# Attention scores of a head pair issued in one place, on two halves of TensorE's rows

## The chip, the cores and the metric

The kernel runs on one core of a Trainium2 chip. The metric is the device time of one execution in microseconds (us); smaller is better. Five engines work beside each other and wait for each other through semaphores: TensorE (PE, matrix products, with its weight loads shown as PEld), VectorE (DVE), ScalarE (ACT), GpSimd (POOL) and SyncE (SP, which issues the DMAs here). Products land in PSUM, which has eight banks of 128 partitions by 512 fp32 values.

## The reference, cut to what matters

The program computes two model blocks, one after the other, on 512 tokens of width 1024. The change concerns only the first mixer of the first block, an attention by "stick breaking" with 16 heads of width 64:

```python
q, k, v = jnp.split(h @ w_in, 3, axis=-1)            # 512 x 1024 each, 16 heads of 64
for start in range(0, seq, QBLK):                    # QBLK = 128: four blocks of queries
    end = start + QBLK
    z = jnp.einsum('bhtd,bhsd->bhts', qf[:, :, start:end], kf[:, :, :end]) * scale
    earlier = jnp.arange(end)[None, :] < jnp.arange(start, end)[:, None]
    log_keep = jnp.where(earlier, jax.nn.log_sigmoid(-z), 0.0)
    csum = jnp.cumsum(log_keep, axis=-1)
    log_w = jax.nn.log_sigmoid(z) + (csum[..., -1:] - csum)
    w = jnp.where(earlier, jnp.exp(log_w), 0.0)
    outs.append(jnp.einsum('bhts,bhsd->bhtd', w, vf[:, :, :end]))
```

Everything else (cross attention, feed-forward, the three branches of the second block) is the same before and after, and takes more than four fifths of the time.

## The kernel before

**Numbers in two parts.** All large products run with fp32 operands that are split into a high part (rounded to fp32r) and a low part (the rest). `mm3` sums three products: high by high, low by high, high by low. A split costs one ACT copy (high) and one subtraction, on DVE mostly (low).

**Pairs of heads.** The attention goes through eight pairs `hp` of heads. For each pair, two GEMMs over xT (24 matmuls of 512 columns each, `chunk`) give q and k of both heads, transposed: head e stands in rows `hrow(e)`, 64 rows each. Four `gemm_v` per two pairs give the values. `gemm_q` writes one tile per head, with the head's high part in its own 64 rows and its low part in the other 64. `gemm_k` writes per head a tile with the high part in both halves, and another with the low part in the head's own half and zeros in the other (`k_lo`). So one matmul over all 128 rows sums two of the three products, and a second one the third: 2 matmuls for a head and a block of queries (`scores`, line 482).

**The chain of a pair**, in the generator `attention` (line 480): scores (PE) into a PSUM bank, a sigmoid (`keep`, ACT), a cumulative product (`r`, a scan on DVE), the difference of neighbours (`w`, POOL); this five times (`weights_of`: block 1 of both heads together, then for each head blocks 0 and 2 together and block 3). Then 20 transposes of w on PE in five groups, each group followed by a split (`wth` on ACT, `wtl` on DVE); then 16 matmuls with v (`values`), and the sums of the two parts (`yt`, `y`), and their split.

**What sets the order.** Each engine runs its instructions in the order in which the program records them. The generator is run beside the GEMMs: `mm` counts the columns of the GEMM matmuls, and during the attention every 1650 ns of them by its own count (8 matmuls of 512 columns, 16 of 256) `tick` lets the generator go on to its next `yield`; the number that it yields (table `WAIT`, at0 to at5) is how many ticks it then waits. `tick` also calls `pump`, which issues the next load of weights (`wr`, two buffers) and records the conversion of the one loaded (`wh` on ACT, `wl` on DVE, lines 144 and 145). Attention of pair hp runs beside the GEMMs of pair hp+1: beside q, k and then two `gemm_v` where hp is 0, 2 or 4; beside two `gemm_v`, q and k where hp is 1, 3 or 5. `drain` finishes it before the next begins. Pair 6 runs beside q and k of pair 7, and pair 7 beside GEMMs over `memT` (256 columns, split into `kT`); there pair 6's rest is not drained first, so the two pairs overlap.

**PSUM.** Eight banks in four rings: g (3 banks, GEMMs), a (2), b (2), c (1).

## Time and profile before

| | |
|---|---|
| median of 3 runs | 1349.75 us (1348.98 to 1350.78) |
| the profiled execution | 1349.54 us, of which the span of the trace is 1347.8 us |
| TensorE busy | 1322.6 us, 98% of the span |
| granted TensorE clock | full in every slice of the page |
| attention (with its GEMMs) | from the start to about 222 us |

A busy PE is not a PE at its peak: matmuls are pipelined, and the duration of one (272 to 400 ns) holds a tail that the next one covers. What a matmul costs in a stream is the distance from its start to the start of the next one, and that is how the rows below are to be read.

### The profile page before, as it was taken

The numbers are of one execution on the slowest core, as the hardware profiler recorded it, in microseconds if no ns is written. First come the engines' busy times: TensorE is split into PE (matmuls) and PEld (weight loads), VectorE is DVE, ScalarE is ACT, GpSimd is POOL, SyncE is SP. The second block draws the span as 40 slices with busy tenths as digits, with TensorE's granted clock in tenths as the row PEclk, the third lists the DMA queues.
The fourth block names the chain that finished last, engine by engine and source line by source line (L and its number), as shares of the span: only waits on it lengthen the run. The fifth ranks groups of instructions, "written<-read, shape, count | busy, mean of one in ns | idle before, by whom it ended". The sixth has DMA issues, their size and how long they took to land.

```text
span 1347.8 us, 19442 instructions
## 1 busy us (share of the span) xinstructions
PE 1322.6 (98%) x7804; PEld 1108.6 (82%) x7804; DVE 833.7 (62%) x1428; ACT 527.2 (39%) x780; POOL 248.1 (18%) x241
## 2 busy tenths in 40 slices
PE   8999999999999999999999989999999989999997
PEld 7988888778879888888888888888877768887886
DVE  5787887865577665523456775767235666743575
ACT  6565665144423533421345136443222454222230
POOL 1433432000000433310133121200000442000220
PEclk9999999999999999999999999999999999999999
DMA  5221343242223322232234212233222223322341
GB/s 191 64 91 53 103 153 125 79 155 96 78 79 111 124 94 94 94 109 94 94 125 141 78 63 94 75 111 98 91 79 79 71 77 93 110 94 68 110 152 63
DMA packets 54666, 133.25 MB, mean 99 GB/s; under 512 B 19632, under 2 KB 21552, under 8 KB 54576
## 3 DMA queue, kind: packets, MB, share of 16 engines
q1 hardware_dynamic: 54576, 132.01, 30.2%
q8 instruction: 61, 1.00, 0.3%
q14 instruction: 29, 0.24, 0.1%
HBM read 126.48 MB, written 5.24 MB: 98 GB/s over the span
## 4 chain that ended last, share of the span: by engine, by line
PE 85%; DVE 9%; ACT 3%; issue 1%; DMA 1%; POOL 0%; DVEq 0%; SPq 0%; ACTq 0%; POOLq 0%
PE ps_chunk L214 48%; PE ps_rows L214 9%; PE ps_d L214 6%; PE ps_br L214 5%; PE ps_v L214 4%; PE ps_lead L214 3%; DVE wl L145 2%; PE ps_s L488 1%; PE ps_o L542 1%; DVE lnt L650 1%; PE ps_t L510 1%; PE ps_z L214 1%; PE ps_o L214 1%; DVE rs_t L279 1%; PE ps_w L1214 1%
## 5 line engine op out<-in xcount | busy, mean ns | idle before, releaser
L145 DVE TENSOR_TENSOR wl<-wr,wh 128x1024 fp32r<-128x1024 f32 x196 | 255.6, 1305 | 141.2 <-ACT wh L144 140.5
L144 ACT CAST wh<-wr 128x1024 fp32r<-128x1024 f32 x196 | 204.8, 1046 | 114.4 <-PE ps_d L214 51.2
L214 PE MATMUL ps_chunk<-h3Tl,wh 128*128 128x512 f32 x480 | 124.6, 395 | 0.0
L214 PE MATMUL ps_chunk<-h3Th,wh 128*128 128x512 f32 x480 | 124.5, 395 | 0.0
L214 PE MATMUL ps_chunk<-h3Th,wl 128*128 128x512 f32 x480 | 124.5, 396 | 0.0
L872 DVE SCALAR_TENSOR_TENSOR c<-ps_chunk,colp,c 128x511 f32<-128x511 f32 x80 | 59.9, 749 | 87.8 <-ACT c L870 86.4
L878 POOL TENSOR_TENSOR c<-c 128x512 f32<-128x512 f32 x21 | 42.4, 2021 | 363.4 <-ACT c L877 209.0
L214 PEld LDWEIGHTS ps_chunk<-h3Th,wh 128*128 128x128 f32 x480 | 89.0, 188 | 20.1 <-issue 1.5
L214 PEld LDWEIGHTS ps_chunk<-h3Th,wl 128*128 128x128 f32 x480 | 89.8, 189 | 19.0 <-issue 0.2
L214 PEld LDWEIGHTS ps_chunk<-h3Tl,wh 128*128 128x128 f32 x480 | 89.1, 188 | 19.3 <-issue 0.8
L214 PE MATMUL ps_chunk<-h2Th,wh 128*128 128x512 f32 x320 | 79.1, 389 | 0.0
L214 PE MATMUL ps_chunk<-h2Tl,wh 128*128 128x512 f32 x320 | 79.0, 389 | 0.0
L214 PE MATMUL ps_chunk<-h2Th,wl 128*128 128x512 f32 x320 | 79.0, 389 | 0.0
L500 POOL TENSOR_TENSOR w<-r 128x511 f32<-128x511 f32 x40 | 58.7, 1468 | 84.7 <-DVE r L498 75.9
L870 ACT ACTIVATE c<-ps_chunk,colp 128x512 f32<-128x512 f32 x40 | 31.1, 778 | 110.3 <-PE ps_chunk L214 110.3
L214 PEld LDWEIGHTS ps_chunk<-h2Tl,wh 128*128 128x128 f32 x320 | 60.1, 188 | 12.5
L214 PEld LDWEIGHTS ps_chunk<-h2Th,wl 128*128 128x128 f32 x320 | 60.1, 188 | 12.5
L214 PEld LDWEIGHTS ps_chunk<-h2Th,wh 128*128 128x128 f32 x320 | 60.0, 188 | 12.4
L498 DVE TENSOR_TENSOR_SCAN r<-keep,masks 128x512 f32<-128x512 f32 x40 | 59.8, 1509 | 12.5 <-ACT keep L496 8.0
L214 PE MATMUL ps_chunk<-xTh,wh 128*128 128x512 f32 x128 | 35.4, 401 | 4.8 <-ACT xTh L376 4.8
L214 PE MATMUL ps_d<-wh,gvb 128*128 128x512 f32 x128 | 39.8, 389 | 0.0
L496 ACT ACTIVATE keep<-ps_s 128x512 f32<-128x512 f32 (+1 forms) x48 | 24.5, 525 | 37.8 <-PE ps_s L488 37.8
(397 smaller groups left out, 2611.0 us busy)
## 6 DMA issues: line engine op xcount, KB each, us to landing
wr<-in_w_in_dram SPq DMA_DIRECT2D x65, 512.0 KB, 3.5
wr<-in_w_ff_dram SPq DMA_DIRECT2D x44, 512.0 KB, 3.5
wr<-in_w_dn_dram SPq DMA_DIRECT2D x22, 512.0 KB, 3.4
wr<-in_w_qk_dram SPq DMA_DIRECT2D x14, 512.0 KB, 3.5
wr<-in_w_br_dram SPq DMA_DIRECT2D x12, 512.0 KB, 3.4
wr<-in_w_v_dram SPq DMA_DIRECT2D x8, 512.0 KB, 3.5
wr<-in_w_xk_dram SPq DMA_DIRECT2D x8, 512.0 KB, 3.9
wr<-in_w_o_dram SPq DMA_DIRECT2D x8, 512.0 KB, 3.4
```

The lines of the kernel that those rows point to most:

```text
L144: A.copy(w.hi, raw)
L145: lo_of.tensor_tensor(w.lo, raw, f32(w.hi), ALU.subtract)
L214: T.matmul(ps, l, r, start=start, stop=stop)
L279: V.scalar_tensor_tensor(t, y, nv, y, ALU.mult, ALU.mult)
L488: T.matmul(ps[:, o:o + n], q[e][:, tok(i)], part[:, 0:n], start=z == 0 and o == 0, stop=z == 1 and i == parts[-1][1])
L496: A.activation(keep[:, j * n:(j + 1) * n], ps[:, 0:n], AF.Sigmoid, scale=-0.125)
L498: V.tensor_tensor_scan(r[:, ::-1], keep[:, ::-1], masks[:, m, ::-1], 1.0, ALU.mult, ALU.max)
L500: G.tensor_tensor(t[:, 0:S - 1], r[:, 1:S], r[:, 0:S - 1], ALU.subtract)
L510: T.transpose(ps[:, n], src[:, o + j * P:o + (j + 1) * P], ident)
L870: A.activation(c, ps, AF.Identity, scale=cw(2), bias=col("ffb", j))
L872: V.scalar_tensor_tensor(c[:, 2 - r:S], ps[:, 0:S - 2 + r], cw(r), c[:, 2 - r:S], ALU.mult, ALU.add)
L878: (V if end else G).tensor_tensor(cv, cg, cv, ALU.mult)
```

## The change

- `gemm_qk` replaces `gemm_q` and `gemm_k`: one split of the whole chunk, 128 rows at a time, into a high and a low tile. Nothing is stacked or doubled, and the zeroed `k_lo` tiles are gone.
- `scores` takes one head's 64 rows as they are, and so needs three matmuls for a head and a block (high by high, high by low, low by high) where two did. The heads take turns: each matmul of head 0, on rows 0 to 63 of the array, is followed by the same one of head 1, on rows 64 to 127, into another bank.
- All scores of a pair are recorded in one place, into six banks (a, a, b, b, c, g). The five sigmoids, scans and differences are recorded there too, one behind the other, where two to three GEMM groups lay between them before.
- The transposes come in two places, 8 and 12 (before 8, 4 and 8), and both heads' values in one, in banks c and g.
- `WAIT`: five ticks between scores and transposes, one between the two places of transposes, two before the values.

```diff
@@ -60,7 +60,7 @@
     "quant": 1550, "turn1": 7, "turn2": 6, "sn0": 1, "sn1": 4, "sn2": 5, "sn3": 3, "st0": 5, "st1": 4, "st2": 5, "st3": 4,
     "gate": 4, "p1": 2, "p2": 5, "p3": 4, "p4": 4, "ac": 2, "tk": 2, "inv": 1, "invn": 2, "pw0": 4, "pw1": 4,
     "pw2": 6, "pw3": 7, "mx": 4, "ysp": 1, "gl": 1, "xc": 14, "x1": 1, "x2": 2, "x3": 2, "so": 2, "mp": 2, "pp": 3,
-    "ss": 2, "us": 3, "ye": 4, "yo": 3, "yt": 1, "at0": 1, "at1": 1, "at2": 1, "at3": 1, "at4": 1,
+    "ss": 2, "us": 3, "ye": 4, "yo": 3, "yt": 1, "at0": 1, "at1": 1, "at2": 5, "at3": 1, "at4": 2,
     "at5": 2, "mh0": 2, "mh1": 3, "mh2": 1, "mh3": 2, "mh4": 1, "mix": 2, "as7": 2, "qa": 1650, "as": 1,
 }
 
@@ -429,37 +429,13 @@
         G.affine_select(out=masks[:, m, o:o + P], in_=masks[:, m, o:o + P], pattern=[[-1, P]],
                         compare_op=ALU.is_gt, fill=1.0, base=0, channel_multiplier=1)
 
-    def qk_tile(name):
-        return att("qk", 7, name, dt=F32R)
-
-    k_lo = [at.tile([P, S], F32R, name=f"kl{e}") for e in range(2)]
-    for e in range(2):
-        A.mul(k_lo[e][hrow(1 - e)], masks[hrow(1 - e), 0], 0.0)
-
-    def gemm_q(ps=None):
+    def gemm_qk(ps=None):
 
         if ps is None:
             ps = chunk(xT)
-        q = [qk_tile("q") for _ in range(2)]
-        for e in range(2):
-            A.copy(q[e][hrow(e)], ps[hrow(e)])
-        for e in range(2):
-            own = hrow(e)
-            V.tensor_tensor(q[e][hrow(1 - e)], ps[own], f32(q[e][own]), ALU.subtract)
-        return q
-
-    def gemm_k(ps=None):
-
-        if ps is None:
-            ps = chunk(xT)
-        k = [Split(qk_tile("kh"), lo) for lo in k_lo]
-        for o in range(2):
-            for e in range(2):
-                A.copy(k[e].hi[hrow((e + o) % 2)], ps[hrow(e)])
-        for e in range(2):
-            own = hrow(e)
-            V.tensor_tensor(k[e].lo[own], ps[own], f32(k[e].hi[own]), ALU.subtract)
-        return k
+        s = Split(att("qk", 8, "qkh", dt=F32R), att("qk", 8, "qkl", dt=F32R))
+        split_from(ps, s.hi, s.lo)
+        return s
 
     vws = []
 
@@ -480,13 +456,17 @@
     def attention(hp, q, k, vs):
         w, wT = {}, {}
 
-        def scores(e, *parts):
-
-            for z, part in enumerate((k[e].hi, k[e].lo)):
-                for ps, i, o in parts:
+        def scores(tags, *parts):
+
+
+            pss = [bank(t, "ps_s") for t in tags]
+            for z, (l, r) in enumerate(((q.hi, k.hi), (q.hi, k.lo), (q.lo, k.hi))):
+                for i, o in parts:
                     n = (i + 1) * P
-                    T.matmul(ps[:, o:o + n], q[e][:, tok(i)], part[:, 0:n],
-                             start=z == 0 and o == 0, stop=z == 1 and i == parts[-1][1])
+                    for e in range(2):
+                        T.matmul(pss[e][:, o:o + n], l[hrow(e), tok(i)], r[hrow(e), 0:n],
+                                 start=z == 0 and o == 0, stop=z == 2 and i == parts[-1][0])
+            return pss
 
         def weights_of(pss, m):
 
@@ -511,51 +491,34 @@
                 wT.setdefault((e, j), (s, n))
             split_from(ps.rearrange("p a b -> p (a b)"), s.hi, s.lo)
 
-        pss = [bank("a", "ps_s") for _ in range(2)]
+        pss = [scores(*parts) for parts in (("aa", (1, 0)), ("bb", (0, 0), (2, P)), ("cg", (3, 0)))]
+        t = weights_of(pss[0], 2)
+        w[0, 1], w[1, 1] = (t, 0), (t, 256)
         for e in range(2):
-            scores(e, (pss[e], 1, 0))
-        t = weights_of(pss, 2)
-        w[0, 1], w[1, 1] = (t, 0), (t, 256)
-        yield wait["at0"]
-        for e in range(2):
-            ps = bank("a", "ps_s")
-            scores(e, (ps, 0, 0), (ps, 2, P))
-            t = weights_of([ps], 0)
+            t = weights_of(pss[1][e:e + 1], 0)
             w[e, 0], w[e, 2] = (t, 0), (t, P)
-            yield wait["at0"]
-            ps = bank("a", "ps_s")
-            scores(e, (ps, 3, 0))
-            w[e, 3] = (weights_of([ps], 1), 0)
-            yield wait["at1"] if e == 0 else wait["at2"]
-
-        def values(e):
-            ps = bank("ca"[e], "ps_o")
-            steps = []
-            for j in range(4):
-                s, n = wT[e, j]
-                wid = (4 - j) * P
-                lhs = vs[j][:, hp % 2, 2 * e:2 * e + 2, :].rearrange("p a d -> p (a d)")
-                steps += [(z, j, lhs, part[:, n * P:n * P + wid]) for z, part in enumerate((s.hi, s.lo))]
-            steps.insert(3, steps.pop(7))
-            steps.insert(6, steps.pop(7))
-            for z, j, lhs, part in steps:
-                T.matmul(ps[:, j * P:S], lhs, part, start=(j == 0 and z == 0), stop=j == 2 and z == 1)
-            own, oth = hrow(e), hrow(1 - e)
-            A.copy(tmp[own], ps[oth])
-            V.tensor_tensor(y[own], ps[own], tmp[own], ALU.add)
-
+            w[e, 3] = (weights_of(pss[2][e:e + 1], 1), 0)
+        yield wait["at2"]
         group("b", [(0, i, 0) for i in range(4)])
         group("b", [(0, 1, 1), (0, 2, 1), (0, 3, 1), (0, 3, 3)])
         yield wait["at3"]
         group("a", [(0, 2, 2), (0, 3, 2), (1, 2, 2), (1, 3, 2)])
-        yield wait["at3"]
+        group("a", [(1, 1, 1), (1, 2, 1), (1, 3, 1), (1, 3, 3)])
         group("b", [(1, i, 0) for i in range(4)])
-        group("a", [(1, 1, 1), (1, 2, 1), (1, 3, 1), (1, 3, 3)])
+        yield wait["at4"]
         y, tmp = att("y", 1, "y"), att("keep", 2, "yt")
-        yield wait["at4"]
-        values(0)
-        yield wait["at5"]
-        values(1)
+        order = [(z, j) for j in range(4) for z in range(2)]
+        order.insert(3, order.pop(7))
+        order.insert(6, order.pop(7))
+        for e in range(2):
+            ps = bank("cg"[e], "ps_o")
+            for z, j in order:
+                s, n = wT[e, j]
+                T.matmul(ps[:, j * P:S], vs[j][:, hp % 2, 2 * e:2 * e + 2, :].rearrange("p a d -> p (a d)"),
+                         (s.hi, s.lo)[z][:, n * P:n * P + (4 - j) * P], start=(z, j) == (0, 0), stop=(z, j) == order[-1])
+            own, oth = hrow(e), hrow(1 - e)
+            A.copy(tmp[own], ps[oth])
+            V.tensor_tensor(y[own], ps[own], tmp[own], ALU.add)
         split_to(y, yT.hi[:, hp], yT.lo[:, hp])
 
     memT = bigt("memT", [P, 2, KC, M])
```

On PE, the scores of pair 1 in the stretch where the attention of pair 1 starts beside `gemm_v` of pair 2. Before (`q` holds high and low of one head, `kh` and `kl` the two tiles of k):

```order
L214 MATMUL ps_v<-wh,xTh 128x256 x8
L488 MATMUL ps_s<-kh,q 128x256
L488 MATMUL ps_s<-kl_158,q 128x256
L488 MATMUL ps_s<-kh,q 128x256
L488 MATMUL ps_s<-kl_159,q 128x256
L214 MATMUL ps_v<-wl,xTh 128x256 x8
L214 MATMUL ps_v<-wh,xTl 128x256 x8
L488 MATMUL ps_s<-kh,q 128x128
L488 MATMUL ps_s<-kh,q 128x384
L488 MATMUL ps_s<-kl_158,q 128x128
L488 MATMUL ps_s<-kl_158,q 128x384
L214 MATMUL ps_chunk<-xTh,wh 128x512 x8
```

and now, where `qkh` and `qkl` are the high and low tiles of q and of k:

```order
L467 MATMUL ps_s<-qkl,qkh 128x256 x2
L467 MATMUL ps_s<-qkh,qkl 128x256 x2
L467 MATMUL ps_s<-qkh 128x128 x2
L467 MATMUL ps_s<-qkh 128x384 x2
L467 MATMUL ps_s<-qkl,qkh 128x128 x2
L467 MATMUL ps_s<-qkl,qkh 128x384 x2
L467 MATMUL ps_s<-qkh,qkl 128x128 x2
L467 MATMUL ps_s<-qkh,qkl 128x384 x2
L467 MATMUL ps_s<-qkh 128x512 x2
L467 MATMUL ps_s<-qkl,qkh 128x512 x2
L467 MATMUL ps_s<-qkh,qkl 128x512 x2
L214 MATMUL ps_chunk<-xTh,wl 128x512 x8
```

The 16 matmuls that stood in five places between GEMM groups are 24 in one, and "x2" is one matmul of each head.

On DVE, from the scores of pair 1 to its last subtraction for the values. Before (an `r` row is a scan; the listing calls it SCALAR_TENSOR_TENSOR):

```order
L498 SCALAR_TENSOR_TENSOR r<-keep,masks 128x512 x2
L477 TENSOR_TENSOR v<-ps_v,v 128x2x128
L498 SCALAR_TENSOR_TENSOR r<-keep,masks 128x512
L145 TENSOR_TENSOR wl<-wr,wh 128x1024
L498 SCALAR_TENSOR_TENSOR r<-keep,masks 128x512
L145 TENSOR_TENSOR wl<-wr,wh 128x1024
L498 SCALAR_TENSOR_TENSOR r<-keep,masks 128x512
L448 TENSOR_TENSOR q<-ps_chunk,q 64x512 x2
L233 TENSOR_TENSOR wtl<-ps_t,wth 128x512 x2
L145 TENSOR_TENSOR wl<-wr,wh 128x1024
L233 TENSOR_TENSOR wtl<-ps_t,wth 128x512 x3
```

and now:

```order
L478 SCALAR_TENSOR_TENSOR r<-keep,masks 128x512 x5
L453 TENSOR_TENSOR v<-ps_v,v 128x2x128
L145 TENSOR_TENSOR wl<-wr,wh 128x1024 x2
L233 TENSOR_TENSOR qkl<-ps_chunk,qkh 128x512
L233 TENSOR_TENSOR wtl<-ps_t,wth 128x512 x2
L145 TENSOR_TENSOR wl<-wr,wh 128x1024
L233 TENSOR_TENSOR wtl<-ps_t,wth 128x512 x3
```

Between the scans stood a split of v and two conversions of weights (`wl`); now these stand behind all five scans, and q's subtraction is one of 128 rows where it was two of 64.

On ACT, the same stretch. Before:

```order
L496 ACTIVATE keep<-ps_s 128x256 x2
L496 ACTIVATE keep<-ps_s 128x512
L476 CAST v<-ps_v 128x2x2x64
L496 ACTIVATE keep<-ps_s 128x512
L144 CAST wh<-wr 128x1024
L496 ACTIVATE keep<-ps_s 128x512
L144 CAST wh<-wr 128x1024
L496 ACTIVATE keep<-ps_s 128x512
L445 CAST q<-ps_chunk 64x512 x2
L232 CAST wth<-ps_t 128x512 x2
L144 CAST wh<-wr 128x1024
L232 CAST wth<-ps_t 128x512 x3
```

and now:

```order
L476 ACTIVATE keep<-ps_s 128x256 x2
L476 ACTIVATE keep<-ps_s 128x512 x4
L452 CAST v<-ps_v 128x2x2x64
L144 CAST wh<-wr 128x1024 x2
L232 CAST qkh<-ps_chunk 128x512
L232 CAST wth<-ps_t 128x512 x2
L144 CAST wh<-wr 128x1024
L232 CAST wth<-ps_t 128x512 x3
```

The conversions `wh` stood among the sigmoids; now two stand behind all of them, and the third still stands ahead of the last three `wth`.

## Rows read from the trace of the kernel before

**Rows 1.** The page: engines' busy us, share of the span, instructions.

```profile
PE 1322.6 (98%) x7804; PEld 1108.6 (82%) x7804; DVE 833.7 (62%) x1428; ACT 527.2 (39%) x780; POOL 248.1 (18%) x241
```

**Rows 2.** Stretches: us, busy PE, PEld, DVE, ACT, POOL (instructions), PEclk, DMA share, GB/s.

```profile
11.00:195.00 184.00, 183.94 (x1139) 165.13 (x1138) 143.76 (x163) 113.09 (x194) 62.12 (x80) 1.00 0.29 93
195.00:222.00 27.00, 24.56 (x190) 23.43 (x190) 23.52 (x28) 14.84 (x27) 9.37 (x11) 1.00 0.46 159
```

**Rows 3.** Waits of PE, up to 222 us: for whom, us, times, longest.

```profile
PE ps_t L510 <- POOL w L502: 1.4, 1, 1.4
PE ps_s L488 <- DVE wtl L233: 0.5, 1, 0.5
PE ps_s L488 <- ACT keep L496: 0.5, 1, 0.5
```

**Rows 4.** Timeline, pair 1's scores and the GEMMs among them: start, length, engine, instruction.

```profile
56.93 1.12 PE L214 MATMUL ps_v<-wh,xTh 128*128 128x256 f32 x8
...
57.89 0.28 PE L488 MATMUL ps_s<-kh,q 128*128 128x256 f32 x1
...
58.36 1.10 PE L214 MATMUL ps_v<-wl,xTh 128*128 128x256 f32 x8
...
60.26 0.45 PE L488 MATMUL ps_s<-kh,q 128*128 128x128 f32 x2
...
60.83 2.01 PE L214 MATMUL ps_chunk<-xTh,wh 128*128 128x512 f32 x8
...
62.68 0.40 PE L488 MATMUL ps_s<-kh,q 128*128 128x512 f32 x1
...
63.15 1.98 PE L214 MATMUL ps_chunk<-xTl,wh 128*128 128x512 f32 x8
```

**Rows 5.** Timeline of PE, second block: matmuls on alternate halves of 64 rows.

```profile
816.71 1.13 PE L1040 MATMUL ps_wa<-wa,wup 64*128 64x512 f32 x4
817.77 0.51 PE L214 MATMUL ps_lead<-h3Tl,wh 128*128 128x256 f32 x2
...
853.50 1.16 PE L1111 MATMUL ps_ac<-misc,kb 64*128 64x128 f32 x16
854.60 0.66 PE L1066 MATMUL ps_ri<-ident,rb 128*128 128x128 f32 x4
```

**Rows 6.** Timeline of PE: eight matmuls of the same columns on all 128 rows.

```profile
802.11 1.05 PE L664 MATMUL ps_hT<-diag,hp 128*128 128x128 f32 x8
802.92 0.72 PE L214 MATMUL ps_lead<-h3Th,lead_w 128*128 128x256 f32 x4
```

**Rows 7.** Timeline: a scan on DVE without, two with POOL's subtraction beside them.

```profile
59.15 1.23 DVE L498 TENSOR_TENSOR_SCAN r<-keep,masks 128x512 f32<-128x512 f32 x1 [1.19 <-ACT keep L496]
...
66.44 1.94 DVE L498 TENSOR_TENSOR_SCAN r<-keep,masks 128x512 f32<-128x512 f32 x1
...
69.42 2.06 DVE L498 TENSOR_TENSOR_SCAN r<-keep,masks 128x512 f32<-128x512 f32 x1
```

**Rows 8.** Timeline: conversions of weights, splits of transposes, pair 1's values.

```profile
65.20 1.20 DVE L145 TENSOR_TENSOR wl<-wr,wh 128x1024 fp32r<-128x1024 f32 x1
...
71.28 1.06 ACT L144 CAST wh<-wr 128x1024 fp32r<-128x1024 f32 x1
...
74.74 1.04 PE L510 MATMUL ps_t<-ident,w 128*128 128x128 f32 x8
75.26 2.02 DVE L233 TENSOR_TENSOR wtl<-ps_t,wth 128x512 fp32r<-128x512 f32 x3
...
75.53 0.48 PE L542 MATMUL ps_o<-wth,v 128*128 128x512 f32 x1
...
76.89 0.39 PE L542 MATMUL ps_o<-wth,v 128*128 128x512 f32 x1
...
83.23 1.47 DVE L145 TENSOR_TENSOR wl<-wr,wh 128x1024 fp32r<-128x1024 f32 x1 [1.64 <-ACT wh L144]
```

**Rows 9.** The page: DMA issues, KB each, median us from issue to landing.

```profile
wr<-in_w_qk_dram SPq DMA_DIRECT2D x14, 512.0 KB, 3.5
```

6 lines of the change are left out of this document (3 added, 3 removed).

## The prediction

> **What bounds the kernel now.** I read the page first: PE is busy for 98% of the span [rows 1]. Then the stretches: while attention runs beside GEMMs, from 11 to 195 us, PE is idle for 0.06 us of 184; in the tail beside memT, for 2.4 us of 27 [rows 2], and the list of waits names the same 2.4 us (1.4 + 0.5 + 0.5) [rows 3]. So a microsecond of matmul time saved in attention is a microsecond gained, and one that DVE, ACT or POOL saves is worth nothing by itself. The other way round, each microsecond by which another engine is now late is lost in full, since nothing idles on PE to take it up. How near the others are is told by no share of busy time; it has to be walked along their queues, below.
>
> The sum is made against the profiled execution (1349.54 us; the median of the three runs is 1349.75).
>
> **The scores: fewer passes, if the halves run together.** Now: the four matmuls of 256 columns take 58.36 - 57.89 = 0.47 us, one head's blocks 0 and 2 (128 and 384 columns, two passes) 60.83 - 60.26 = 0.57, one head's block 3 (512) 63.15 - 62.68 = 0.47 [rows 4]. A pair costs 0.47 + 2 x 0.57 + 2 x 0.47 = 2.55 us. One pass of one head is 0.118 + 0.285 + 0.235 = 0.638. After: three passes, and each of them serves both heads if the halves of the array work at once: 3 x 0.638 = 1.91. The gain is 0.64 a pair, **5.1 us** for eight. If they do not, 6 x 0.638 = 3.83, a loss of 1.28 a pair, 10.2 in all.
>
> The second block shows halves of 64 rows by turns already: 16 matmuls of 128 columns, two heads alternating, are followed by the next instruction 854.60 - 853.50 = 1.10 us after the first [rows 5]. Eight of 128 columns on all rows need 802.92 - 802.11 = 0.81, 0.10 each [rows 6]. One behind the other the 16 would need 1.6 us; as eight pairs 0.81. So pairs do run at once there, and 1.10 - 0.81 = 0.29 us are left over, which I take for going into the half-row mode and out of it. Four of 512 columns take 817.77 - 816.71 = 1.06 [rows 5]; less the same 0.29 that is 0.39 for a pair, and a lone one would be some 4 x 0.10 = 0.40. These are fp32 operands, not fp32r, so both ends stay (gain 5.1, loss 10.2); I take 5.1, since the nearest rows are halves of the same kind.
>
> **The switch** costs 8 x 0.29 = **2.3 us** (0 if it hid behind another wait, 4.6 if it doubled). That it is paid once for each pair is what issuing all scores in one place buys.
>
> TensorE's clock is no matter: it is granted in full now (PEclk 1.00) [rows 2], and PE stays nearly without gaps. Transposes (20) and value matmuls (16) are the same in number.
>
> **The queues: what five scans in a row hold up.** DVE and ACT have fewer splits of q and k (two subtractions in place of four, two casts in place of six); alone that is worth nothing. But the scans move together, and what stood between them comes after. I walk pairs 1, 3 and 5 (beside gemm_v, q and k), T being the start of the scores.
>
> DVE: the first scan starts 59.15 - 57.89 = 1.3 us after the first score [rows 4, 7]. A scan alone takes 1.23, beside a subtraction of POOL 1.94 to 2.06 [rows 7]; now each of scans 2 to 5 has the subtraction of the one before it beside it. Five take 1.2 + 4 x 2.0 = 9.2: T + 10.5 (at 1.23 each it would be T + 7.5). Behind them v's split of 256 columns (0.4, estimated from 2.02 for three of 512 [rows 8]), then the first conversion of weights, 1.20 alone and 1.47 with POOL at work [rows 8]; the fifth subtraction is beside it: T + 12.4. That frees the buffer of raw weights, and only now SP can load the next: 3.5 us to landing [rows 9], T + 15.9. ACT's cast of it (1.06) stands in ACT's queue ahead of the last three `wth`: T + 17.0. On DVE its `wl` (1.20) stands ahead of the last three `wtl` (2.02 together) [rows 8]: T + 20.2.
>
> PE: scores with the switch 2.2; 16 matmuls of 256 at 0.12 (0.96 for eight [rows 4]) T + 4.1; q's 24 of 512 at 0.23, T + 9.6; k's first eight T + 11.5; eight transposes (0.79 [rows 8]) T + 12.3; eight T + 14.1; twelve transposes T + 15.3; eight T + 17.2; the values of head 0 (76.89 - 75.53 = 1.36 [rows 8]) and one matmul of head 1: T + 18.8. The next needs the third `wtl`: it waits 20.2 - 18.8 = 1.4. Three pairs: **4.2 us** (0 with scans at 1.23; 2.5 each if the first conversion waits for POOL longer).
>
> Pair 0 stands beside q and k, then v: PE needs v's second kind of weights at T + 2.2 + 1.9 + 5.5 + 1.0 = T + 10.6; their `wl` comes right behind the scans: T + 10.5 + 1.5 = T + 12.0. **1.5 us** (0 to 2). In pairs 2 and 4 v's weights are converted earlier, and the same walk leaves DVE done by T + 18, PE needing it at T + 18.8: nothing.
>
> **The tail** (pair 7): pair 6's values of head 1 go to a g bank that the fifth sigmoid of pair 7 still has to read; with two `keep` buffers that sigmoid waits for the third scan, T + 1.3 + 1.2 + 4.0 = T + 6.5, and takes some 0.6 (1.06 for ACT's 1024 columns [rows 8]). PE is there at T + 2.2 + 1.9 + 1.4 = T + 5.5: a wait of 1.6. Then a GEMM over memT wants a bank whose `kT` split stands behind the five scans, for some 0.7 more. The two waits of 0.5 go, that of 1.4 for the last transposes stays. 1.6 + 0.7 - 1.0 = **1.3 us** (0 to 3).
>
> **Sum:** -5.1 + 2.3 + 4.2 + 1.5 + 1.3 = +4.2 us; 1349.5 + 4.2 = **1353.7 us**.
>
> **Rivals.**
> (A) The queues keep up and the change gains. It decides on the distance of the scans: at 1.65 us in place of 2.0 the chain of pairs 1, 3 and 5 comes 1.4 earlier and their wait is gone, as is nearly all of pair 0's; what is left is -5.1 + 2.3, so 1346.7. For it: scans alone are 1.23, and the mean of rows with partial cover lies between. Against it: both rows that met POOL are at 1.94 or more.
> (B) The halves do not run at once with fp32r: +10.2 for the scores; PE comes 1.9 us later to each wait, so those of pairs 0, 1, 3 and 5 vanish; with the tail 1349.5 + 10.2 + 1.3 = 1361. Against it: rows 5.
> (C) The halves run at once, but long pairs take longer than one: if the 1.06 us of rows 5 holds no switch, a pair of 512 columns is 0.53 against 0.40, 1.3 times. Then the scores are 0.3 x 15.3 = 4.6 us dearer and the switch (2.3) is not there: 2.3 more, half of it hidden in the four waits: 1354.9. Against it: by rows 5 and 6 the short pairs leave 0.29 as well, and that is the same sum once, not in proportion to the columns (0.29 of 0.81, and 0.29 of 0.77). The Trainium skill, "TensorE: Matmul & The Clock Gate", Part 3 (Measured speedup vs the span model), speaks for it: it gives 3.07 times for four row tiles at 512 columns, not 4, an estimate of 4/3.07 = 1.3 lone passes for a packed set. No run here has yet shown fp32r halves.
> (D) The waits are there, but half as large (the DMA lands sooner, or the first conversion does not meet POOL): 1353.7 - 3 = 1350.7, within what can be measured. This is the low part of the forecast.
>
> **How the numbers follow.** A measurement of this kernel can tell about 0.2% (2.7 us) from no change: faster is below 1346.8, slower above 1352.2. The forecast with (D), 1350 to 1357.5, has 0.66, of which 0.43 lies above 1352.2 and 0.23 below. (A), between 1345 and 1349, has 0.24: 0.15 faster, 0.09 same. (B) 0.05, (C) 0.05, both slower. Faster 0.15, same 0.32, slower 0.53. The range runs from 1346.5, where the half of (A) that gains most is left out, to 1358, beyond which lie (B) and a few per cent of the forecast. The forecast's own range is 1350 to 1357.5.
>
> **What the profile after would show.** The 24 scores of a pair in 2.2 us to the next GEMM (over 3.8 under B, 2.5 without any gap at the ends under C); the five scans of a pair 2.0 us apart (below 1.7 under A); PE waiting for `wtl` in three places and once for `wl`, together some 5 to 6 us, in the stretch that has 0.06 us of idle PE now; ACT idle for a load of weights just ahead of the last `wth`. If PE shows no idle time from 11 to 195 us, the walk along the queues is wrong; if the scores do not shrink by 5 us, the step on the halves is.

## The result

The changed kernel takes **1361.4 us** (median of four runs, 1360.4 to 1362.2), the kernel before, beside it, 1350.3 (four runs, 1349.0 to 1352.2): slower, by a ratio of 1.0083 (95% interval 1.0070 to 1.0096). The forecast was 1353.7 with a range up to 1358.0, so the sign was right and the size was not. In the comparisons further down, with 13 to 21 runs each, the kernel before has medians of 1350.95 to 1351.6, so the distance is rather 10 us than 11.

The stretch beside GEMMs in the changed kernel, which answers to the first of [rows 2] (us, busy PE, PEld, DVE, ACT, POOL with their instructions, granted clock, DMA share, GB/s):

```profile
11.00:195.00 184.00, 178.02 (x1145) 154.92 (x1144) 125.57 (x138) 90.78 (x153) 64.27 (x74) 1.00 0.26 83
```

PE was idle for 0.06 us from 11 to 195; now it is idle for 6.0, while DVE and ACT are less busy than before (125.6 and 90.8 us against 143.8 and 113.1; a few per cent of that because less work fits in). So no engine has become too slow; work comes in the wrong order. For whom PE waits up to 235 us, as [rows 3] (us, times, longest):

```profile
PE ps_o L517 <- DVE wtl L233: 3.7, 6, 0.7
PE ps_t L490 <- DVE wtl L233: 2.9, 4, 1.5
PE ps_chunk L214 <- DVE kT L233: 1.7, 1, 1.7
PE ps_o L517 <- ACT keep L476: 1.1, 1, 1.1
PE ps_v L214 <- DVE wl L145: 0.9, 1, 0.9
```

Most of these waits are of the kinds that the walk along the queues had named. The timeline of pair 1, which stands against [rows 4, 7, 8] (start, length, engine, instruction, and in brackets how long the engine was idle before it and who ended that; neighbours of one kind are one row, and a view of fewer instructions parts them):

```profile
59.12 0.39 PE L467 MATMUL ps_s<-qkh 64*128 64x256 f32 x2
...
59.34 0.28 PE L467 MATMUL ps_s<-qkl,qkh 64*128 64x256 f32 x2
...
60.43 0.40 PE L467 MATMUL ps_s<-qkh 64*128 64x512 f32 x2
...
60.59 2.34 DVE L478 TENSOR_TENSOR_SCAN r<-keep,masks 128x512 f32<-128x512 f32 x2 [1.49 <-ACT keep L476]
60.66 0.39 PE L467 MATMUL ps_s<-qkl,qkh 64*128 64x512 f32 x2
...
61.21 1.21 PE L214 MATMUL ps_v<-wl,xTh 128*128 128x256 f32 x8
...
61.95 1.80 POOL L480 TENSOR_TENSOR w<-r 128x511 f32<-128x511 f32 x1 [3.22 <-DVE r L478]
...
65.88 1.23 DVE L478 TENSOR_TENSOR_SCAN r<-keep,masks 128x512 f32<-128x512 f32 x1 [0.87 <-POOL w L480]
...
66.00 1.94 POOL L480 TENSOR_TENSOR w<-r 128x511 f32<-128x511 f32 x1
...
67.94 1.03 POOL L480 TENSOR_TENSOR w<-r 128x511 f32<-128x511 f32 x1
67.98 2.08 DVE L478 TENSOR_TENSOR_SCAN r<-keep,masks 128x512 f32<-128x512 f32 x1 [0.87 <-POOL w L482]
...
70.20 1.04 POOL L480 TENSOR_TENSOR w<-r 128x511 f32<-128x511 f32 x1 [1.06 <-DVE r L478]
...
70.30 2.03 DVE L145 TENSOR_TENSOR wl<-wr,wh 128x1024 fp32r<-128x1024 f32 x1
...
72.35 1.46 SPq L123 DMA_DIRECT2D wr<-in_w_v_dram  x2
...
74.71 0.33 PE L490 MATMUL ps_t<-ident,w 128*128 128x128 f32 x1 [0.46 <-DVE wtl L233]
...
76.06 1.05 ACT L144 CAST wh<-wr 128x1024 fp32r<-128x1024 f32 x1 [3.85 <-DMA wr<-in_w_v_dram]
...
78.28 1.88 DVE L233 TENSOR_TENSOR wtl<-ps_t,wth 128x512 fp32r<-128x512 f32 x3
...
79.02 0.38 PE L517 MATMUL ps_o<-wtl,v 128*128 128x256 f32 x1 [0.70 <-DVE wtl L233]
...
80.22 0.50 PE L517 MATMUL ps_o<-wtl,v 128*128 128x512 f32 x1 [0.58 <-DVE wtl L233]
```

Read it from the top: the 24 scores take 2.09 us to the next GEMM, and two matmuls of 512 columns, one of each head, start every 0.23 us. The third, fourth and fifth scan each begin after 0.87 us of idle time that POOL ends. The first conversion of weights comes at 70.30, just behind the start of POOL's last subtraction (70.20), and takes 2.03; at its end SP issues the next load (72.35), whose data ACT casts at 76.06, ahead of the last three `wth`; their `wtl` follow, and PE stands still three times.

**Where the time lies.** In start times, not idle times, since a wait also leaves the tail of the matmul before it uncovered: from pair 0's first score to the first product over yT the kernel before has 192.8 us, the changed one 201.2 us, 8.45 more. By pairs (from the start of one pair's scores to those of the next), before and after, pairs 0 to 5: 24.15, 23.93, 24.16, 23.93, 24.67, 23.93 against 25.29, 25.96, 23.93, 25.99, 23.93, 25.88; pairs 6 and 7 together 48.01 against 50.25. With 0.25 us a pair gained by the scores (below), the rest of each is what was lost:

| step of the prediction | forecast, us | measured, us |
|---|---|---|
| scores and switch, eight pairs | -2.8 | -2.0 (8 x 0.25) |
| pair 0 | +1.5 | +1.4 |
| pairs 1, 3, 5 | +4.2 | +6.8 |
| pairs 2 and 4 | 0 | -0.5 |
| tail (pairs 6 and 7) | +1.3 | +2.7 |
| attention | +4.2 | +8.45 |
| behind the attention | 0 | +3.1 in these two executions |

The -0.5 is pair 4 of the kernel before, whose value matmuls stretch by that much in both its traces. The list of PE's waits does not show it, since the tail of the matmul before covers nearly all of it; the weight loads (PEld) show it. In the first trace two of them wait for `wtl`, 0.38 us here and 0.30 at 150.02:

```profile
149.42 0.19 PEld L542 LDWEIGHTS ps_o<-wtl,v 128*128 128x128 f32 x1 [0.38 <-DVE wtl L233]
```

In that pair DVE has a conversion `wl` (147.55, 1.22 us) right ahead of the last two `wtl`; in pair 2 it has none there. So the kernel before already had, in one pair, the kind of wait that the change brings to pairs 1, 3 and 5.

### The profile page after: what moved, and what is told of

Its sections match the earlier page's. It is cut to its first block, busy times and chain, and to the rows that moved or that the text cites. A ratio compares the mean times of both kernels' runs of the same rounds, so it can differ in the third digit from the quotient of the medians.

```text
span 1359.4 us, 19502 instructions
## 1 busy us (share of the span) xinstructions
PE 1323.6 (97%) x7868; PEld 1104.1 (81%) x7868; DVE 814.6 (60%) x1412; ACT 508.8 (37%) x746; POOL 257.6 (19%) x241
## 4 chain that ended last, share of the span: by engine, by line
PE 78%; DVE 10%; DMA 4%; ACT 3%; POOL 2%; issue 2%; DVEq 0%; SPq 0%; POOLq 0%; ACTq 0%
PE ps_chunk L214 43%; PE ps_rows L214 9%; PE ps_d L214 6%; PE ps_br L214 5%; PE ps_v L214 3%; PE ps_lead L214 3%; DVE wl L145 3%; POOL w L480 2%; ACT wh L144 1%; PE ps_o L517 1%; DVE lnt L613 1%; DMA wr<-in_w_xq_dram 1%; PE ps_z L214 1%; PE ps_o L214 1%; PE ps_ac L1074 1%
## 5 line engine op out<-in xcount | busy, mean ns | idle before, releaser
L480 POOL TENSOR_TENSOR w<-r 128x511 f32<-128x511 f32 x40 | 63.0, 1576 | 67.0 <-DVE r L478 67.0
L478 DVE TENSOR_TENSOR_SCAN r<-keep,masks 128x512 f32<-128x512 f32 x40 | 55.0, 1390 | 28.3 <-POOL w L480 13.9
L214 PEld LDWEIGHTS ps_chunk<-h2Th,wh 128*128 128x128 f32 x320 | 60.0, 188 | 12.4
L1260 POOL TENSOR_TENSOR misc<-misc,rs_y 128x256 f32<-128x256 f32 x8 | 6.5, 842 | 160.2 <-DVE rs_y L285 160.2
```

Of the source, the lines that this page charges most:

```text
L214: T.matmul(ps, l, r, start=start, stop=stop)
L478: V.tensor_tensor_scan(r[:, ::-1], keep[:, ::-1], masks[:, m, ::-1], 1.0, ALU.mult, ALU.max)
L480: G.tensor_tensor(t[:, 0:S - 1], r[:, 1:S], r[:, 0:S - 1], ALU.subtract)
L1260: G.tensor_tensor(yt[:, q, :, e], yt[:, q, :, e], ri[:, e, q].unsqueeze(2).to_broadcast([P, NT, CH]), ALU.mult)
```

## The experiments: the five scans in a row

Beside each time stand the ratio to the kernel before, run on the same chip, and the length of the attention as above (192.8 us before, 201.2 changed).

**Scans one tick apart, first order.** In pairs 0 to 6:

```diff
-        for e in range(2):
-            t = weights_of(pss[1][e:e + 1], 0)
-            w[e, 0], w[e, 2] = (t, 0), (t, P)
-            w[e, 3] = (weights_of(pss[2][e:e + 1], 1), 0)
-        yield wait["at2"]
+        for m, part in ((1, 2), (0, 1)):
+            for e in range(2):
+                yield 1
+                t = weights_of(pss[part][e:e + 1], m)
+                ...
+        yield wait["at2"] - 4
```

> The changed kernel with one thing undone: the scores stay in one place, but the sigmoid, scan and difference of a set are recorded one tick apart, as before, in pairs 0 to 6 (block 1, then block 3 of both heads, then blocks 0 and 2); pair 7 is left as it is. Theory (five scans in a row hold up the conversions behind them): the waits of the values in pairs 1, 3 and 5 (2.2 us each by the trace of after) and that of pair 0 (1.1) go, so 1361.4 - 6.6 - 1.1 = about 1353.7 us; pair 1 then lasts 23.9 - 0.46 = 23.5 us from its scores to those of pair 2, where it lasts 25.96 now. Rival (the waits come from the transposes and values standing together, in two places and one): they stay, 1361. If both have a share, between.

Measured: 1359.6 us (1.0064, 1.0049 to 1.0079), attention 200.0. Neither: the waits for `wtl` are gone from 11 to 195 us, but another stands there:

```profile
PE ps_t L490 <- POOL w L482: 6.3, 6, 1.6
```

The order here is block 1, then block 3 of both heads, then blocks 0 and 2 of both; the first transposes need head 0's blocks 0 and 2, which come last but one. Pairs 1, 3 and 5 fall from 25.9 to 24.8 us, pairs 2 and 4 rise from 23.9 to 25.0. That is a fault of the order that I chose, so the next version has the order of the kernel before.

**Scans one tick apart, order of the kernel before.** The same yields between the sets, blocks 0 and 2 of head 0 second, and banks that allow it:

```diff
-(("aa", (1, 0)), ("bb", (0, 0), (2, P)), ("cg", (3, 0)))
+(("aa", (1, 0)), ("gb", (0, 0), (2, P)), ("cb", (3, 0)))
```

> The changed kernel with its two buffers for a scan's result, and the five sets of sigmoid, scan and difference one tick apart in pairs 0 to 6, in the order of the kernel before (blocks 0 and 2 of head 0 second): the version that held 184.00 of 184 us on PE without its third buffer. Theory (five scans in a row are the cause, the buffers only decide how long the row is): still no wait for a split in pairs 0 to 6, each pair 23.5 to 24 us, and the tail as in the changed kernel at worst: 1351 to 1353 us. Rival (the third buffer did it): waits of about 1 us in pairs 1, 3 and 5, 1355 us.

Measured: 1351.3 us (1.0003, 0.9994 to 1.0012), attention 191.6. Pairs 23.93 and 23.55 us by turns, and in the stretch of [rows 2]:

```profile
11.00:195.00 184.00, 184.00 (x1222) 163.12 (x1222) 136.52 (x152) 95.71 (x164) 64.43 (x80) 1.00 0.32 101
```

So the waits of pairs 0, 1, 3 and 5 come from recording the five scans in a row: scores and values stand in one place here too, with two scan buffers. The banks were exchanged along with it, and no run does that alone; but the first order kept the changed kernel's banks and had no wait for `wtl` in this stretch either, and the next version keeps banks and order both.

**A third buffer for a scan's result**, the order of the changed kernel untouched:

```diff
-            r = att("r", 2, "r")
+            r = att("r", 3, "r")
```

> The changed kernel with three buffers for the result of a scan in place of two, the order of instructions unchanged. By the trace of after, the third, fourth and fifth scan of a pair each stand idle 0.87 us until POOL has read the buffer two scans back. Theory (the distance of the scans is that wait for a buffer, and the rest of the chain hangs on it): the fifth scan ends 2.5 us earlier, the waits of pairs 0, 1, 3 and 5 go (1.1 and 3 x 2.2), and the tail, whose sigmoid and split stand behind the same scans, loses some 2 of its waits: 1361.4 - 9.7 = about 1352 us. Rival (POOL's subtraction and the scan slow each other by what they use together, so an earlier start is paid back by longer scans, 2.0 us each): the fifth scan ends less than 1 us earlier, at most 3 us gained, 1358 to 1361.

Measured: 1352.4 us (1.0009, 0.9999 to 1.0018), attention 192.7. The rows of all scans from 11 to 195 us (busy us, mean ns, and the idle time before them by who ended it), of the changed kernel and of this one:

```profile
L478 DVE TENSOR_TENSOR_SCAN r<-keep,masks 128x512 f32<-128x512 f32 x35 | 48.1, 1391 | 25.7 <-POOL w L480 12.1 <-ACT keep L476 7.5 <-POOL w L482 6.1
```

```profile
L478 DVE TENSOR_TENSOR_SCAN r<-keep,masks 128x512 f32<-128x512 f32 x35 | 56.6, 1680 | 7.5 <-ACT keep L476 7.5
```

The 18.2 us of waiting for POOL are gone; half of them come back as longer scans, since they now meet the subtraction (this is the rival's part). In pair 1 the five take 8.08 us in place of 9.47:

```profile
60.10 8.08 DVE L478 TENSOR_TENSOR_SCAN r<-keep,masks 128x512 f32<-128x512 f32 x5 [1.49 <-ACT keep L476]
...
68.41 1.68 DVE L145 TENSOR_TENSOR wl<-wr,wh 128x1024 fp32r<-128x1024 f32 x1
...
73.74 1.05 ACT L144 CAST wh<-wr 128x1024 fp32r<-128x1024 f32 x1 [2.02 <-DMA wr<-in_w_v_dram]
```

The scores start at 58.63 here, so the chain's cast comes 15.1 us behind them, where it came 16.9 behind (76.06 - 59.12): 1.4 earlier for the scans, 0.4 for the first conversion. That is nearly enough, because PE was only some 2 us too early: up to 195 us PE still waits 0.6 us for `wtl` and 0.3 for `wl`. One buffer of 2 KB a partition is worth 9 of the 10 us.

**Both**: three buffers and scans one tick apart.

> The changed kernel with three buffers for a scan's result and the five sets of sigmoid, scan and difference one tick apart in pairs 0 to 6, in the order of the kernel before (blocks 0 and 2 of head 0 second), the score banks swapped for that. Theory (the cost is the five scans in a row): no wait is left in pairs 0 to 6, and pairs 1, 3 and 5 last 23.9 us or less; against the version with three buffers alone it gains the 0.6 us of waits for the values and what pair 0 still waits: 1351.3 us. Rival (scores issued in one place need their scans in one place, since PE comes to the transposes before the last difference, as in the first spread version): 1 us more in a pair, 1358.

Measured: 1350.8 us (0.9994, 0.9985 to 1.0004), attention 190.5, 2.3 less than before, pairs 23.93 and 23.55, PE busy for 184.00 of 184. It is the best version, and no difference from the kernel before can be measured.

**Transposes and values later.**

```diff
-"at3": 1, "at4": 2,
+"at3": 2, "at4": 3,
```

> The changed kernel with two numbers of its table changed: two ticks in place of one between the two places of transposes, three in place of two before the values; two scan buffers as it has. Nothing becomes faster, the waiting matmuls only come two ticks later, behind GEMMs that wait for nothing. Theory (PE comes to the values before the splits that five scans have held up): the waits of pairs 1, 3 and 5 (0.6 at the third group of transposes, 0.8 and 0.75 at the values) go, 6.3 in all, and the 1.5 us of the tail's transposes in part; pair 0's wait for v's weights stays: 1361.4 - 6.3 = about 1355 us, 1353.5 if the tail gains too. Rival (the queues of DVE and ACT are too full in a pair, so that a later place only moves the wait): 1361.

Measured: 1368.9 us (1.0123, 1.0106 to 1.0141), attention 208.0: the theory falls, the rival too, it is worse by 7.5. PE at the end of pair 1:

```profile
74.26 1.98 PE L214 MATMUL ps_chunk<-xTh,wl 128*128 128x512 f32 x8
76.08 1.47 PE L490 MATMUL ps_t<-ident,w 128*128 128x128 f32 x12
77.31 0.48 PE L517 MATMUL ps_o<-wth,v 128*128 128x512 f32 x1
...
80.06 0.38 PE L517 MATMUL ps_o<-wtl,v 128*128 128x256 f32 x1 [0.93 <-DVE wtl L233]
```

No GEMM stands between the transposes and the values any more. A pair has nine ticks (three for each product of 512 columns, one and a half for each `gemm_v`), and the changed kernel's waits use all of them: its values already come right behind the last GEMM. What is put off beyond that is run by `drain` in one piece, with nothing beside it. I had not counted the ticks. The version with three buffers, at3 = 2 and head 1's values in ring a met the same end of the pair:

```diff
-"at3": 1,
+"at3": 2,
-            ps = bank("cg"[e], "ps_o")
+            ps = bank("ca"[e], "ps_o")
```

> The changed kernel with three buffers for a scan's result, two ticks between the two places of transposes, and the values of head 1 in a bank of ring a, as before, in place of ring g. Theory (with three buffers what is left stands in the tail: 1.0 us of the values behind pair 7's fifth sigmoid, which reads the g bank, and 1.4 of the third group of transposes behind its split): both go, and 0.6 of the waits in the pairs: 1352.4 - 2.5 = about 1350 us. Rival (the tail is bound by the conversions of weights and of kT on DVE, and PE meets them one matmul later): 1352.

Measured: 1356.8 us (1.0038, 1.0025 to 1.0051), attention 194.2; PE waits 1.8 us for `wtl` in six places, pairs 1 to 5 last 24.1 to 24.5 us. What it was meant to tell of the tail it does not tell.

## The experiments: the halves of the rows

**Heads one behind the other.** The loop over e goes outside:

```diff
-            for z, (l, r) in enumerate(...):
-                for i, o in parts:
-                    for e in range(2):
+            for e in range(2):
+                for z, (l, r) in enumerate(...):
+                    for i, o in parts:
```

> The changed kernel with the heads' scores one behind the other in each set, not by turns: the same matmuls on the same rows, 24 in a pair. Theory (the two halves of the rows run at once when the heads take turns): a pair's scores take 2.09 + 1.91 = 4.0 us; the waits of pairs 0, 1, 3 and 5, which count from the start of the scores, take up 1.1 + 3 x 1.9 of the eight times 1.91, so 1361.4 + 15.3 - 6.8 = about 1370 us. Rival (a matmul on 64 rows is shorter by itself and the turns give nothing): the scores stay at 2.1 us and the time at 1361.

Measured: 1361.2 us (1.0076, 1.0059 to 1.0093), attention 201.6. Neither: the scores take 2.50 us (59.35 to 61.85), 0.41 more, not 1.9. Pairs 2 and 4 last 24.30 us where they lasted 23.93; in pairs 1, 3 and 5 the waits hide it (25.86, 25.78, 25.91). The records of the last set (three matmuls of 512 columns for head 0, then three for head 1):

```profile
60.67 0.39 PE L467 MATMUL ps_s<-qkh 64*128 64x512 f32 x1
...
60.90 0.39 PE L467 MATMUL ps_s<-qkl,qkh 64*128 64x512 f32 x1
61.06 0.39 PE L467 MATMUL ps_s<-qkh 64*128 64x512 f32 x1
61.13 0.39 PE L467 MATMUL ps_s<-qkh,qkl 64*128 64x512 f32 x1
61.30 0.39 PE L467 MATMUL ps_s<-qkl,qkh 64*128 64x512 f32 x1
61.53 0.39 PE L467 MATMUL ps_s<-qkh,qkl 64*128 64x512 f32 x1
61.85 0.39 PE L214 MATMUL ps_v<-wl,xTh 128*128 128x256 f32 x1
```

The halves overlap all the same (a record does not name its head; whose it is follows from the order of the three products): head 0 goes on at 60.67, 60.90 and 61.13, head 1 at 61.06, 61.30 and 61.53, each at a lone head's pace of 0.23, and head 1's first starts before head 0's third, which stands ahead of it in the program. So turns are not what makes them run at once; neighbourhood is.

**One head a place.** The kernel before, its places and order, with the changed kernel's operands:

```diff
-            for z, part in enumerate((k[e].hi, k[e].lo)):
+            for z, (l, r) in enumerate(((q.hi, k.hi), (q.hi, k.lo), (q.lo, k.hi))):
...
-                    T.matmul(ps[:, o:o + n], q[e][:, tok(i)], part[:, 0:n], ...
+                    T.matmul(ps[:, o:o + n], l[hrow(e), tok(i)], r[hrow(e), 0:n], ...
```

> The kernel before with its places and its order, but with the changed kernel's operands: one split of q and k, three matmuls on a head's own 64 rows for a head and a block. So no other head's matmul stands beside them in four of the five places. Theory (what a half gains comes from the other half running at once): a pair's scores take six passes where full rows take four, 3.83 us and five times a switch of some 0.2, against 2.53: 2.3 us more in a pair, 18 in all, nothing hides it, 1369 us. Rival (64 rows are quicker by themselves): 1351 or less.

Measured: 1374.6 us (1.0170, 1.0154 to 1.0185), attention 213.5, pairs of 27.1 and 26.8 us, 2.9 more each. The theory holds; the switch was taken too small. A place with block 3 alone, which takes 0.47 us on full rows [rows 4]:

```profile
65.63 1.07 PE L214 MATMUL ps_chunk<-xTh,wh 128*128 128x512 f32 x4
66.62 0.49 PE L464 MATMUL ps_s<-qkh 64*128 64x512 f32 x1
...
67.51 0.73 PE L214 MATMUL ps_chunk<-xTl,wh 128*128 128x512 f32 x2
```

Three passes of 0.235 would be 0.70; from first to next GEMM it is 0.89, and 0.09 more lie ahead of the first.

**Three places.** The version with three buffers and scans one tick apart, with the scores of each set, both heads by turns, one tick apart:

```diff
-        pss = [scores(*parts) for parts in places]
+        pss = [scores(*places[0])]
...
+            if e == 0:
+                pss.append(scores(*places[1]))
...
+            if e == 0:
+                pss.append(scores(*places[2]))
```

> The version with three buffers and scans one tick apart, with the scores in three places, one tick apart too, both heads by turns in each: block 1, then blocks 0 and 2, then block 3. Theory (each going into the half-row mode and out of it costs by itself, 0.3 us by the kernel with one head a place: 2.9 more a pair, of which 1.3 are passes and the rest five places): two places more are 0.6 us a pair, 8 pairs, 1350.8 + 4.8 = about 1355 us (pair 7 keeps its scans in a row, but its scores then stand together too, so 4.2 for seven pairs: 1355.0). Rival (the switch hides behind the loading of the next weights where GEMMs are on both sides): 1351.

Measured: 1359.0 us (1.0060, 1.0044 to 1.0075), attention 198.9. Pairs 2 and 4 last 24.76 in place of 23.93: 0.83 for two places, 0.42 each, not 0.3. Pairs 1, 3 and 5 last 25.3, of which some 0.6 are a new wait of the transposes for POOL. One place for all scores is worth having.

**Full rows in the changed kernel's place.** The scores of the kernel before, with its `gemm_q` and `gemm_k`, recorded where the changed kernel records them, first under its own order, then with scans one tick apart:

```diff
+            for e in range(2):
+                for z, r in enumerate((k[e].hi, k[e].lo)):
+                    for i, o in parts:
+                        T.matmul(pss[e][:, o:o + n], q[e][:, tok(i)], r[:, 0:n], ...
```

> The changed kernel with the scores of the kernel before (one tile per head, high and low part stacked on 128 rows, two matmuls for a head and a block), but recorded in the changed kernel's one place, with its order of everything else: the move without the halves. Theory (the move costs, the halves gain): a pair's scores 2.55 in place of 2.09 us; in pairs 2, 4 and 6, which do not wait, 0.46 each in full, in the others the wait takes up part of it, while the additional splits of q and k on 64 rows (0.67 us each on DVE, two more in a pair) stand ahead of the splits that the values wait for and add up to 0.7 each: 1361.4 + 1.4 + 0 to 3 = 1363 to 1366 us. Rival (the halves are what costs): near the kernel before, 1350 us.

Measured: 1361.3 us (1.0080, 1.0065 to 1.0095), attention 203.7 against 201.2. The move without the halves costs the same 10 us: the rival falls. The 1363 to 1366 of the theory are not reached either: the attention is 2.5 longer, but in this execution the part behind it is 2.4 shorter (1113.6 against 1116.0).

> The version with two scan buffers and scans one tick apart, with the scores of the kernel before (128 rows, two matmuls for a head and a block, high and low stacked) in the same one place: only the operands of the scores differ, and the splits of q and k behind them. By the traces a pair's scores take 2.53 us on full rows and 2.10 + 0.09 on halves. Theory (PE never waits there, so the 0.34 us show in full): pairs 2 and 4 last 23.93 + 0.34 = 24.27 us, eight pairs 2.7 us, 1351.3 + 2.7 = 1354 us. Rival (the halves' gain is lost in the GEMM behind them): the same pair lengths, 1351.

Measured: 1352.9 us (1.0015, 1.0006 to 1.0024) against 1351.3 (1.0003) with halves: between the two. (The attention, 196.0 us, is 4.5 longer; what the pairs below leave of that lies in the tail, where both wait 3.1 us for kT and the granted clock behind that is lower for longer here.) Where PE never waits, pairs last 24.15 and 23.80 us against 23.93 and 23.55: the halves gain 0.22 to 0.25 a pair, not 0.34. Here are the edges, with halves and with full rows:

```profile
83.34 0.39 PE L467 MATMUL ps_s<-qkh,qkl 64*128 64x512 f32 x2
83.66 1.21 PE L214 MATMUL ps_chunk<-xTh,wl 128*128 128x512 f32 x4
```

```profile
83.88 0.39 PE L491 MATMUL ps_s<-kl,q 128*128 128x512 f32 x1
84.11 0.85 PE L214 MATMUL ps_chunk<-xTh,wl 128*128 128x512 f32 x3
```

From the last score to the GEMM it is 0.32 in place of 0.23, and four GEMM matmuls behind it take 1.21 where three take 0.85: less the tail of 0.39, 0.82 for three steps against 0.46 for two, so the three steps have 0.11 more than 3 x 0.235.

## The experiments: the tail, and the part behind the attention

With scans in a row in pair 7 and one tick apart elsewhere, one wait is left: that for kT, 1.7 us with three scan buffers, 3.1 with two. Four tries to remove it, each from the version with three buffers and scans one tick apart. Pair 7 one tick apart too:

```diff
-        gap = 0 if hp == NPAIR - 1 else 1
+        gap = 1
-            ps = bank("cg"[e], "ps_o")
+            ps = bank(("aa" if hp == MEM_AT else "cg")[e], "ps_o")
```

> The version with three buffers and scans one tick apart, in pair 7 too, and the values of pair 6 in the two banks of ring a, which pair 7's scores leave first. Theory (its only wait up to the end of the attention is 1.7 us for a split of kT that stands behind pair 7's scans, and the clock fell behind it: eight matmuls of 256 columns took 1.9 us where 1.1 is the rule): both go, 1350.8 - 1.7 - 1.3 = about 1348 us. Rival (spread over more time, pair 7 ends later and the product over yT waits for it): 1351.

Measured: 1353.1 us (1.0011, 1.0002 to 1.0020), attention 193.3.

Pair 7 with three sets and, a tick later, two (and pair 6's values in ring a, as in the last diff):

```diff
-        gap = 0 if hp == NPAIR - 1 else 1
+        last = hp == NPAIR - 1
+        gaps = [0, 0, 1, 0] if last else [1] * 4
```

> The version with three scan buffers and scans one tick apart in pairs 0 to 6, with pair 7's five sets recorded as three and, a tick later, two, and the values of pair 6 in the banks of ring a. kT's second split and the sums of pair 6 then stand behind three scans of pair 7, not five. Theory (the 1.7 us wait for kT, and the lower clock behind it, come from the scans in a row): they go, and the last differences come some 2 us later but ahead of the last transposes: 1350.8 - 2 to 3 = about 1348.5 us. Rival (as in best_tail, the transposes of head 1 then wait for the last difference): 1351 to 1353.

Measured: 1352.0 us (1.0002, 0.9993 to 1.0011), attention 191.7.

Pair 7's scores out of ring g, block 3 second:

```diff
+        places = [("aa", (1, 0)), ("ab" if last else "gb", (0, 0), (2, P)), ("cb", (3, 0))]
+        for n in (0, 2, 1) if last else (0, 1, 2):
+            pss[n] = scores(*places[n])
...
-            ps = bank("cg"[e], "ps_o")
+            ps = bank(("ca" if hp == MEM_AT else "cg")[e], "ps_o")
```

> The version with three scan buffers and scans one tick apart in pairs 0 to 6; pair 7's scans in a row as there, but its scores in banks a, a, c, b, a, b (block 3 second), and pair 6's values in c and a: ring g is left to the GEMMs over memT. Theory (PE meets the late split of kT because pair 7 holds one of the three g banks): with three it may run one product further, 2.9 us, so the wait of 1.7 us goes, and the lower clock behind it: 1350.8 - 1.7 - 1.3 = about 1348 us. Rival (the order on DVE is the cause, whatever the bank): the wait of 1.7 stays or turns up at the last transposes, 1351 us.

Measured: 1352.5 us (1.0006, 0.9997 to 1.0015), attention 191.9.

The same without the last two lines:

> The same with pair 6's values in c and g, as in the changed kernel: one g bank is taken for the 1.4 us of those values and until their sum is read, which stands behind the five scans on ACT and DVE. Theory: that bank comes free late (its sum is read after the scans), so half of the gain is lost, 1349.5 us. Rival: as above, 1351 us.

Measured: 1351.0 us (1.0000, 0.9992 to 1.0009), attention 190.8. What PE waits for from 195 to 230 us, in this order:

```profile
PE ps_t L490 <- POOL w L482: 4.6, 2, 2.5
```

```profile
PE ps_t L490 <- DVE wtl L233: 3.2, 1, 3.2
```

```profile
PE ps_t L490 <- DVE wtl L233: 3.1, 1, 3.1
PE ps_chunk L214 <- DVE kT L233: 0.3, 1, 0.3
```

```profile
PE ps_chunk L214 <- DVE kT L233: 2.0, 1, 2.0
PE ps_t L490 <- DVE wtl L233: 1.5, 1, 1.5
```

The wait for kT does go, or nearly, where the scans are parted, or where ring g is left to the GEMMs altogether, so both theories have something; but in these three versions 3.1 to 4.6 us of waiting turn up at the last transposes, for POOL's last difference or for a `wtl`. In the fourth, where pair 6's values hold a g bank, the wait for kT stays (2.0) and 1.5 us are added. None of these versions beats the kernel before, and how to order this tail better stays open.

**Second traces** of both kernels, unchanged.

> The kernel before, unchanged, for a second trace. From the first matmul over yT to the last of the program its first trace has 1112.9 us, the traces of six changed kernels 1113.6 to 1117.0, though no instruction differs there. Theory (those 1 to 4 us belong to the execution and not to the change: the waits for loads in cross attention and the granted clock in the second block): 1114 to 1116 here. Rival (a later start of that part makes the loads meet otherwise): 1113.

> The changed kernel, unchanged, for a second trace. From pair 0's scores to the first matmul over yT its first trace has 201.2 us (before: 192.8 in both traces), from there to the last matmul 1116.0 (before: 1112.9 and 1115.3). Theory (the attention's part is the change, the rest the execution): 201.2 again, and anything from 1113 to 1117. Rival (the rest is an after-effect of the change): 1116.0 again.

Measured: from pair 0's first score to yT 192.8 us again for the kernel before, 200.6 for the changed one (pairs 1, 3 and 5 at 25.7 us). From yT to the last matmul 1115.3 us for both, where the first traces had 1112.9 and 1116.0. So the two second traces differ in the attention alone, and the profiled execution of before that the prediction started from was a lucky one behind it. The medians are 10 us apart all the same, so up to 2 us there may still belong to the change; no run settles that. Part of the spread is the granted clock: in the second block PE waits some 4 us for DVE, and the 5 us of GEMMs behind that were granted 0.66 of the full clock in the first trace of before (a dip that the page's slices of 34 us do not show), 0.50 (1.2 GHz) in the first of the changed kernel. The second trace of before has 0.69 and 0.63 over ten us there, so the low clock is no mark of the change. The spans of the second traces are 1351.3 and 1358.7 us.

## Why the prediction was right in kind and wrong in size

**The scores were right, their edges a little small.** Passes of both heads at once, 1.91 us, are what the trace has (0.12, 0.285 and 0.23 per step). The switch was taken as 0.29 and is 0.39, in four pieces: 0.09 ahead of the first score, 0.10 behind it (59.12 to 59.34, where 0.12 is the step), 0.09 between the last score and the GEMM, and 0.11 within that GEMM. I read it from [rows 5] as the time to the next instruction, which holds only the two inner pieces. These are 0.19 here, and about 0.20 in [rows 5] too, where a pair of the sixteen has a step of 0.11; the 0.29 came out because the eight of [rows 6] are followed by the next instruction 0.03 us after the last of them, which made them look shorter than eight steps. Left out were the two outer pieces, 0.20. So -2.8 became -2.0.

**The failed step is the sum for pairs 1, 3 and 5**: 4.2 forecast, 6.8 measured, that is 2.3 for each in place of 1.4. The walk was right at every station but late at two, by 0.8 us in all. The scans end at T + 10.9 (forecast 10.5). The first conversion, in the company of POOL's last subtraction, takes 2.03 where I put 1.47, and ends at T + 13.2 (12.4); the cast starts at T + 16.9 (15.9), and the last `wtl` ends at T + 21.0 (20.2). PE would have been there at T + 18.9, as forecast (18.8). The upper bound of 2.5 each, which stood there for just this conversion, comes close to what was measured: 2.3, or 2.4 if pair 1 (25.96) is set against the same pair without a wait (23.55, scans one tick apart). The waits also come in three pieces, since the third group of transposes wants a b bank and each head's values want their own split; in idle time these are 1.7 us for pair 1, in start times 2.2, because each leaves the tail of a matmul uncovered. That is why the list of waits looks as forecast (6.0 us idle from 11 to 195, where I said 5 to 6) and the time does not. Of the 4.2 us that the attention took beyond its forecast, 2.6 belong to these pairs, 1.4 to the tail and 0.8 to the switch; pairs 2 and 4 give 0.5 back. For what stands behind the attention the prediction had no term, and the up to 2 us there stay open.

**A cause was misnamed.** I had each scan 2.0 us long beside a subtraction. The later scans are 2.09 apart, but four of the five are 1.2 long: scans 3 to 5 wait 0.87 for the buffer that POOL still reads, because the subtraction beside a scan takes 1.80 to 1.94 in place of 1.03. The rows that I had, [rows 7], show the other case, a long scan. For the sum it was the same; for the remedy it was not, as a third buffer shows. The Trainium skill, "SBUF — State Buffer" (SBUF: two separate sides), has POOL and a DVE instruction with two inputs in SBUF, as the scan is, take a shared port in turn, the one that starts first keeping it for its instruction; the trace agrees: POOL at 67.94 keeps its 1.03 and the scan at 67.98 takes 2.08, while the scan at 65.88 keeps its 1.23 and the subtraction at 66.00 takes 1.94. (Both end some 0.1 to 0.2 us sooner than if they had begun only when the other was done.)

**Pair 0** (+1.5; its own stations, T + 12.0 and T + 10.6, give 1.4) was met, at +1.4. **The tail** had 1.3 and was 2.7: the fifth sigmoid cost 1.3 (forecast 1.6), the kT split 1.85 (0.7), the two waits of 0.5, in start times 1.3 together, went only by half (-0.7), and 0.1 was added at the last transposes: 2.55 of the 2.7.

**The rivals.** (B) and (C) are out: matmuls of both halves start 0.23 us apart at 512 columns, a lone pass. That (B) named 1361 us, which is what was measured, is luck: its scores grow and its waits vanish, and neither happened. (D) is out as well, since the waits came out larger than forecast and not half as large. The figure of "TensorE: Matmul & The Clock Gate" (Part 3, Measured speedup vs the span model) in the Trainium skill, 3.07 times for four row tiles, does not show with two halves. (A) was right about what decides: with three buffers the scans are 1.62 us apart (8.08 / 5), and from 11 to 195 us only 1.1 us of idle PE are left. It overrated what then remains to be gained: 1352.4 us and not 1346.7.

## To carry to other kernels

When a change puts the same work in one place, follow what stood between the pieces: here five scans in a row delayed a conversion, so a load, so a cast and a split, although DVE and ACT had less to do. Put such chains one tick apart, or give the ring that their consumer holds one buffer more, before paying for the faster matmuls with waits; and take a wait's price from start to start, not from the idle time that a list of waits shows. Before anything is put later, count the ticks that are left until the work beside it ends.
